# Depthwise convolution of a transformer block: from seven tiles on TensorE and one on VectorE to eight on TensorE, with shifted copies made by DMA

## The chip, the cores and the metric

The kernel runs on one core of one Trainium2 chip. The metric is the device time of the execution in microseconds (us). Every run of the kernel before is given below; the profile is of one more execution.

## The reference

Two transformer blocks are computed on 256 positions of 1024 channels, batch 1, in float32. The change lies in the first block, in a conformer convolution module, between its first pointwise product and its second:

```python
def causal_dwconv(x, w):
    k, ch = w.shape
    return lax.conv_general_dilated(
        x, w[:, None, :].astype(x.dtype), window_strides=(1,), padding=[(k - 1, 0)],
        dimension_numbers=("NWC", "WIO", "NWC"), feature_group_count=ch)

def conformer_conv_module(h, w1, b1, dw_w, dw_b, ln_g, ln_b, w2, b2):
    u = h @ w1 + b1
    a, gt = jnp.split(u, 2, axis=-1)
    u = a * jax.nn.sigmoid(gt)
    u = causal_dwconv(u, dw_w) + dw_b
    u = jax.nn.silu(layernorm(u, ln_g, ln_b))
    return u @ w2 + b2

...
    c_act = jax.nn.silu(c)
    mod = c_act @ mod_w[i] + mod_b[i]
    h = rmsnorm(x, norm_pre_mix[i]) * (1.0 + sc_m) + sh_m
```

The convolution has 31 taps per channel. The vector `mod` holds 6 x 1024 scales and shifts; the first two sixths are needed for `h`, the third after the module, the others later. The rest (a feed-forward part with a 3-tap convolution, and a second block with an RWKV mixer, a stick-breaking attention and four more feed-forward parts) is not touched.

## The kernel before

Activations lie with channels on the partitions: a tile is 128 channels x 256 positions, and there are eight (`KD`). Weights stream from HBM in chunks of 1 MB. Since TensorE multiplies in a reduced float32 format here, each half chunk ("unit", 128 x 1024) is split in two: `split_hi` is a cast on ScalarE (L226) and `split_lo` the remainder, a subtraction on VectorE (L235); after every second `split_lo` the next chunk is loaded by SyncE (L204). A product is three matmuls (high x high, high x low, low x high).

The order of the work is the order in which the Python program emits it; every engine runs its own instructions strictly in that order, and so does SyncE with the loads. There is no scheduler.

The matrix behind `mod` is read in 48 tiles `mraw` of 512 KB through five buffers. For each tile VectorE multiplies it with silu(c) (`mod_mult`, L720), ScalarE sums it (`mod_sum`, L724), and then the buffer is loaded again (`mod_load`, L733). One such sum and the next multiply together form a "half" in `mod_later`; halves are put on a list `bg`, and `pump` takes them from it at given places.

The module in the order of its stages:

- First pointwise product, `pw1(k)` for k = 0 to 7 (L1009): 48 matmuls per step into eight PSUM banks. In each step VectorE and ScalarE also make the step's operand (L986, L1031, L1033, L1034, L1045), split two units and do two tiles of `mod`. After step 1 SyncE loads `taps` (L1051); after step 2 GpSimd builds five of the tap matrices `stack` (`conv_stack`, L906, 128 x 1024 each); after step 5 the vectors `vecs` (L663) and the constants are loaded.
- Gate: per tile a sigmoid on ScalarE (L1099) and a multiply on VectorE (L1101) that writes `up`.
- Convolution: tile 0 runs on VectorE in one scaling (L1084) and 30 tap steps (L1088). Tiles 1 to 7 run on TensorE: `shifts` (L1072) multiplies with slices of the identity to bring `up` in four shifts onto the four groups of 32 partitions, ScalarE copies that out of PSUM into `sh` (L1076), and 32 matmuls (L1128) with the tap matrix sum up the taps. ScalarE writes the result with its bias (L1139) and its square (L1331). Two more tap matrices are built when a buffer is free. Between the matmuls `pump` issues 22 halves of `mod` and the tap steps in turn. Five `split_hi` are placed in the last tiles, four `split_lo` after the stage.
- Norm: sums over channels by TensorE (L1383), VectorE and ScalarE make mean and deviation (L1394 to L1405), TensorE broadcasts them (L1408); `keep_warm` issues six filler matmuls before and six after that (L360).
- Second pointwise product: five groups of tiles are normed (L1161), passed through silu (L1167) and split into the operand `xx` (L625, L626). `gemm_square` takes the first four tiles one by one and the last four in `gemm_tail`; the results are read from PSUM on VectorE (L1179), and squared. After the fourth tile `pump` issues the last three halves and the next splits of the memory input `mx`.

Of the kernel before, what the change touches and what calls it, by code (L numbers as in the profile page):

```python
# [23 lines left out]
N_PE_CONV = 7  # L24
N_STACK = 5
MOD_LATE = 3
PUMPS = {3: 3}
CV = (5, 4)
# [3 lines left out]
CONV_ORDER = [4, 5, 0, 1, 2, 3, 6, 7]  # L32
# [218 lines left out]
class Builder:  # L251
# [6 lines left out]
    def __init__(self, ctx, tc, dr, out, parts):  # L258
        self.tc, self.nc, self.dr, self.out = tc, tc.nc, dr, out
        self.parts = parts  # L260
        self.npool = 0
        e = ctx.enter_context
        self.const = e(tc.tile_pool(name="const", bufs=1))
        self.wraw = e(tc.tile_pool(name="wraw", bufs=self.RAW))
        self.whi = e(tc.tile_pool(name="whi", bufs=self.LEAD + 3))
        self.wlo = e(tc.tile_pool(name="wlo", bufs=self.LEAD + 2))
        self.act = e(tc.tile_pool(name="act", bufs=1))
        self.ps_gu = e(tc.tile_pool(name="ps_gu", bufs=2, space=PSUM))
        self.xr = self.act.tile([P, KD, T], F32, name="xr")
# [3 lines left out]
        self.bg = []  # L273
        self.pre = None
# [41 lines left out]
    def enter_dense(self, tmp=True):  # L316

        self.dense = ExitStack()
        self.ps_st = self.dense.enter_context(self.pool("ps_st", PSUM))
        self.ps_acc = self.dense.enter_context(self.pool("ps_acc", PSUM))  # L320
        if tmp:
            self.open_tmp()

# [3 lines left out]
    def leave_dense(self):  # L327
        self.dense.close()
# [408 lines left out]
    def mod_later(self, first, last):  # L737

        def half(n):
            if n > 2 * first:  # L740
                self.mod_sum(self.mod_raw.pop(0), n - 1)
                self.mod_load(1)
            if n < 2 * last:
                self.mod_mult(self.mod_raw[0])

        for n in range(2 * first, 2 * last + 1):
            self.bg.append((1.1, lambda n=n: half(n)))
# [162 lines left out]
    def conformer(self):  # L910
        with self.pool("conf") as cp:
            st, later = self.pointwise_conv(cp)
        self.pointwise_out(st, later)

    def pointwise_conv(self, cp):
# [5 lines left out]
        junk = self.acc_tile(0)[:, 0, :]  # L921
# [76 lines left out]
        npe, ndv = N_PE_CONV, KD - N_PE_CONV  # L998
        first = [j for j in order if j >= ndv]

        banks = [self.acc_tile(i) for i in range(4)] + [self.gu_tile(), self.gu_tile()] + [
# [18 lines left out]
        for k in range(KD):  # L1020
# [39 lines left out]
        ups = [cp.tile([P, (3 if j >= ndv else CW - 1) + T], F32, name=f"up{j}") for j in range(KD)]  # L1060
        for t in ups:
            nc.vector.memset(t[:, :-T], 0.0)

        def shifts(j):

            out = []
            for h in range(2):
                ps = self.gu_tile()
                for s in range(4):
                    for q in range(2):  # L1070
                        c = 64 * h + 32 * q
                        nc.tensor.matmul(ps[32 * s:32 * s + 32, q, :], lhsT=self.k("ident")[:, c:c + 32],  # L1072
                                         rhs=ups[j][:, 3 - s:3 - s + T], start=True, stop=True,
                                         skip_group_check=True)
                sh = cp.tile([P, 2, T], F32, name="sh", bufs=4)
                nc.scalar.copy(out=sh, in_=ps)  # L1076
                out.append(sh)
            return out

        def conv_dve(j):  # L1080
            y = self.ys[:, j, 0, :]

            def first():
                nc.vector.tensor_scalar(out=y, in0=ups[j][:, 0:T], scalar1=self.vec("a_dw_w", j),  # L1084
                                        scalar2=self.vec("a_dw_b", j), op0=ALU.mult, op1=ALU.add)

            def tap(t):
                nc.vector.scalar_tensor_tensor(out=y, in0=ups[j][:, t:t + T],  # L1088
                                               scalar=self.vec("a_dw_w", t * 8 + j), in1=y,
                                               op0=ALU.mult, op1=ALU.add)  # L1090
            return [first] + [lambda t=t: tap(t) for t in range(1, CW)] + [
                lambda: st.square(j, j + 1)]

        taps = []
        sh = {}
        for j in order:
# [4 lines left out]
            nc.vector.scalar_tensor_tensor(out=ups[j][:, -T:], in0=gu[:, 0, :], scalar=self.vec("a_pw1_b", j),  # L1101
                                           in1=sg, op0=ALU.add, op1=ALU.mult)
            if j < ndv:
                taps.append(conv_dve(j))

        self.mod_later(8, 20)
        n = len(self.bg) - MOD_LATE
        mods, later, steps = self.bg[:n], self.bg[n:], list(zip(*taps))
        self.bg = []
        for i, step in enumerate(steps):  # L1110
            for f in step:
                self.bg.append((0.4, f))
            if mods:
                self.bg.append(mods.pop(0))
        for j in range(ndv):
            self.bg.append((0.65, lambda j=j: st.sum(j, j + 1, "dve")))
        self.bg += mods
        self.mark("conv")
        slot = sum(c for c, _ in self.bg) / (4 * npe)
        sh[first[0]] = shifts(first[0])  # L1120
        done = []
        for n, j in enumerate(first):
            if n + 1 < npe:
                sh[first[n + 1]] = shifts(first[n + 1])
            cv = self.acc_tile(n % 4)[:, 0, :]
            for a in range(8):
                for g in range(4):
                    nc.tensor.matmul(cv[32 * g:32 * g + 32, 4 * a:], lhsT=stacks[n][:, 8 * g + a, :],  # L1128
                                     rhs=sh[j][g // 2][:, g % 2, :T - 4 * a], start=a == 0,
                                     stop=a == 7, skip_group_check=True)  # L1130
# [4 lines left out]
            if n + N_STACK < npe:  # L1135
                stacks.append(self.conv_stack(cp, first[n + N_STACK]))
            if done and n < npe - 1:
                st.sum(done[-1], done[-1] + 1, "dve")
# [3 lines left out]
            done.append(j)  # L1142
        self.pump(1000)
        for j in done[-2:]:
            st.sum(j, j + 1, None)
        return st, later

    def pointwise_out(self, st, later):
# [15 lines left out]
        for i, (k0, k1) in enumerate(groups):  # L1164
# [6 lines left out]
            if i in LOS:  # L1171
                self.stream.split_hi()
                self.stream.split_lo()
# [145 lines left out]
class Norm:  # L1319
# [40 lines left out]
    def finish(self, eps, func, ahead=True, fill=(0, 0)):  # L1360
# [6 lines left out]
        b.fill(fill[0], b.WARM0)  # L1367
        bc = next(parts)
        b.fill(fill[1], b.WARM)
# [924 lines left out]
```

## Time and profile before

| | us |
|---|---|
| three runs | 1485.37, 1481.81, 1486.15 |
| median | 1485.37 |
| the profiled execution | 1481.87 |
| span of the profiled execution, first to last instruction | 1480.1 |
| first conv instruction on TensorE | 72.97 |
| broadcast of the norm's values | 125.66 |
| last operand of the second product | 143.11 |
| first read of its result | 148.26 |

The profile lists engines as PE (TensorE), PEld (its weight loads), DVE (VectorE), ACT (ScalarE), POOL (GpSimd) and SP (SyncE, the loads). A timeline row gives the start, the duration, the engine, the line, the operation and the tiles written and read; "x5" means that many instructions in one row, and what stands in square brackets is the idle time before it and what ended it. On VectorE and ScalarE the tail of one instruction overlaps the start of the next by about 0.1 us. PEclk is the granted TensorE clock, 1.00 for 2.4 GHz and 0.50 for 1.2 GHz.

### The profile page before, as it was taken

The page shows a single profiled execution, that of the slowest core. Times are in us where ns is not written, and L with a number is a line of the kernel's source. Part 1 is how long each engine was busy: PE and PEld are TensorE (multiplying, and loading weights), DVE is VectorE, ACT ScalarE, POOL GpSimd, SP SyncE. Part 2 cuts the span into 40 slices and gives each one's busy share as a digit, 9 for nine tenths or more (in the row PEclk, how much of TensorE's full clock was granted, in tenths as well). Part 3 has the DMA queues.
Part 4 walks back from the last instruction along what each step waited for, and adds up shares of the span by engine and source line. Part 5 has one row for each costly group of instructions (what it writes and reads, how often), then busy time and mean ns, then how long its engine had stood idle before and what let it go on. Part 6 is the DMA issues. An engine that isn't in the chain of part 4 may idle for free. (4 is left out here: it accounts for less than half of the span.)

```text
span 1480.1 us, 26075 instructions
## 1 busy us (share of the span) xinstructions
PE 1419.9 (96%) x10664; PEld 1273.4 (86%) x10664; DVE 1076.0 (73%) x1705; ACT 853.8 (58%) x1505; POOL 119.6 (8%) x113
## 2 busy tenths in 40 slices
PE   8888899999999999999999999999999999999997
PEld 7867799998888888898788888888888888888886
DVE  7897788885777656788568776678766765787754
ACT  6787566684655535751346555466554676565542
POOL 1210100001000010031010000110001111100011
PEclk9998899999999999999999999999999999999998
DMA  9774445565355553240024555536554342265540
GB/s 379 292 243 186 170 155 189 198 234 207 136 202 179 196 199 136 86 143 4 2 109 167 184 196 181 189 143 221 182 195 187 136 143 86 91 226 196 196 174 29
DMA packets 39145, 250.38 MB, mean 169 GB/s; under 512 B 4337, under 2 KB 4849, under 8 KB 12274
## 3 DMA queue, kind: packets, MB, share of 16 engines
q1 hardware_dynamic: 38594, 247.60, 45.9%
q8 instruction: 84, 1.38, 0.4%
q10 hardware_dynamic: 432, 1.11, 0.2%
q14 instruction: 35, 0.29, 0.1%
HBM read 247.65 MB, written 1.05 MB: 168 GB/s over the span
## 5 line engine op out<-in xcount | busy, mean ns | idle before, releaser
L235 DVE TENSOR_TENSOR wlo<-wraw,whi 128x1024 fp32r<-128x1024 f32 x416 | 514.3, 1250 | 34.1 <-ACT whi L226 33.4
L226 ACT CAST whi<-wraw 128x1024 fp32r<-128x1024 f32 x416 | 426.3, 1045 | 22.0 <-PE acc L378 5.6
L384 PE MATMUL acc<-hx,whi 128*128 128x512 f32 x880 | 310.7, 398 | 0.0
L384 PE MATMUL acc<-xx,whi 128*128 128x512 f32 x816 | 284.1, 390 | 0.0
L372 PE MATMUL acc<-xx,wlo 128*128 128x256 f32 x1008 | 280.7, 284 | 0.0
L372 PE MATMUL gu<-xx,wlo 128*128 128x256 f32 x1008 | 279.0, 282 | 1.6 <-ACT xx L625 1.0
L372 PE MATMUL acc<-hx,wlo 128*128 128x256 f32 x880 | 247.5, 281 | 0.0
L384 PEld LDWEIGHTS acc<-hx,whi 128*128 128x128 f32 x880 | 165.3, 188 | 40.5
L372 PEld LDWEIGHTS gu<-xx,wlo 128*128 128x128 f32 x1008 | 189.9, 189 | 4.9 <-ACT xx L625 1.7
L372 PEld LDWEIGHTS acc<-xx,wlo 128*128 128x128 f32 x1008 | 190.9, 191 | 0.8
L384 PEld LDWEIGHTS acc<-xx,whi 128*128 128x128 f32 x816 | 153.2, 188 | 32.1
L372 PEld LDWEIGHTS acc<-hx,wlo 128*128 128x128 f32 x880 | 166.1, 189 | 0.0
L384 PE MATMUL gu<-xx,whi 128*128 128x512 f32 x432 | 150.9, 390 | 0.0
L377 PE MATMUL gu<-xx,whi 128*128 128x256 f32 x512 | 148.4, 290 | 2.4 <-ACT u L894 2.4
L378 PE MATMUL gu<-xx,whi 128*128 128x256 f32 x512 | 142.9, 279 | 0.0
L1331 ACT ACTIVATE ys<-ys 128x256 f32<-128x256 f32 (+1 forms) x66 | 28.6, 437 | 151.7 <-DVE ys L1249 134.9
L377 PEld LDWEIGHTS gu<-xx,whi 128*128 128x128 f32 x512 | 96.2, 188 | 10.8 <-issue 7.9
L378 PEld LDWEIGHTS gu<-xx,whi 128*128 128x128 f32 x512 | 96.3, 188 | 0.7 <-issue 0.7
L384 PEld LDWEIGHTS gu<-xx,whi 128*128 128x128 f32 x432 | 81.1, 188 | 17.0
L1348 POOL TENSOR_TENSOR nsum<-ys 128x512 f32<-128x512 f32 (+1 forms) x9 | 12.4, 1380 | 871.1 <-PE acc L384 452.3
L858 ACT COPY lows<-acc 128x256 f32<-128x256 f32 x55 | 20.6, 374 | 97.8 <-PE acc L384 97.6
L1247 DVE SCALAR_TENSOR_TENSOR ys<-xr,acc 128x256 f32<-128x256 f32 x32 | 13.5, 422 | 75.0 <-PE acc L384 75.0
(397 smaller groups left out, 2351.5 us busy)
## 6 DMA issues: line engine op xcount, KB each, us to landing
wraw<-in_w SPq DMA_DIRECT2D x208, 1024.0 KB, 4.8
mraw<-in_mod SPq DMA_DIRECT2D x48, 512.0 KB, 5.5
xr<-in_x SPq DMA_DIRECT2D x2, 512.0 KB, 4.2
m<-in_mem SPq DMA_DIRECT2D x1, 1024.0 KB, 8.2
out<-xr SPq DMA_DIRECT2D x3, 256.0 KB, 2.2
cst<-in_consts SPq DMA_DIRECT2D x1, 546.0 KB
lora<-in_lora ACTq DMA_DIRECT2D x1, 384.0 KB, 3.4
lora_g<-in_lora ACTq DMA_DIRECT2D x1, 384.0 KB, 3.9
```

The lines of the kernel that those rows point to most:

```text
L226: b.nc.scalar.copy(out=hi, in_=raw)
L235: b.nc.vector.tensor_tensor(out=lo, in0=raw, in1=hi.bitcast(F32), op=ALU.subtract)
L372: self.nc.tensor.matmul(out, lhsT=wl, rhs=x[:, 0, :], start=start, stop=False, skip_group_check=True)
L377: mm(out, lhsT=wh, rhs=x[:, 0, :], start=start, stop=False, skip_group_check=True)
L378: mm(out, lhsT=wh, rhs=x[:, 1, :], start=False, stop=False, skip_group_check=True)
L384: self.nc.tensor.matmul(bank, lhsT=wh, rhs=x, start=False, stop=stop, skip_group_check=True)
L858: nc.scalar.copy(out=lows[:, 1, :], in_=banks[1][:, 1, :])
L1247: self.nc.vector.scalar_tensor_tensor(out=y, in0=self.xr[:, k, :], scalar=2 * ALPHA, in1=ps[:, 1, :], op0=ALU.mult, op1=ALU.add)
L1331: b.nc.scalar.activation(out=b.ys[:, k0:k1, 1, :], in_=y, func=AF.Square)
L1348: e.tensor_tensor(out=out[:, q:2, :], in0=prev[:, q:2, :], in1=t[:, q:2, :], op=ALU.add)
```

## The change

All eight tiles are convolved on TensorE, in the order 4, 5, 0, 2, 1, 3, 6, 7. The first three get their shifts from TensorE as before. The other five lie in one tile `upd`, and 16 DMAs of 160 KB (`shifts_dma`, four for each shift) copy it within SBUF into `shd`. Four tap matrices are kept instead of five, and the first four are built after step 6 of the first product; the taps are loaded after step 5, vecs and consts after step 6. silu(c) is copied into two PSUM banks (`pair`) for the multiplies of the convolution stage (`mod_mult_psum`). 18 halves of `mod` are issued there and seven in the second product, two after each of its first four tiles. Three `split_lo` stand between the last conv tiles instead of four after them. The norm's filler matmuls become 18 and 22. The accumulator banks are reopened after the stage.

```diff
-N_PE_CONV = 7
-N_STACK = 5
-MOD_LATE = 3
-PUMPS = {3: 3}
-CV = (5, 4)
+N_STACK = 4
+CONV_ORDER = [4, 5, 0, 2, 1, 3, 6, 7]
+N_DMA = 5
+MOD_LATE = 7
+PUMPS = {0: 2.2, 1: 2.2, 2: 2.2, 3: 2.2}
...
+    def mod_mult_psum(self, raw):
+
+        self.nc.vector.tensor_tensor(out=raw, in0=raw, in1=self.cps, op=ALU.mult)
+
...
+        upd = cp.tile([P, N_DMA, 3 + T], F32, name="upd")
+        ups = [cp.tile([P, 3 + T], F32, name=f"up{n}") for n in range(KD - N_DMA)]
+        for t in ups:
+            nc.gpsimd.memset(t[:, :3], 0.0)
+        nc.gpsimd.memset(upd[:, :, :3], 0.0)
+        ups += [upd[:, n, :] for n in range(N_DMA)]
...
-            if k == 1:
+            if k == 5:
                 nc.sync.dma_start(out=self.taps, in_=self.dr["taps"])
-            elif k == 2:
-                stacks = [self.conv_stack(cp, j) for j in first[:N_STACK]]
-            elif k == 5:
+            elif k == 6:
                 self.load_consts()
+                stacks = [self.conv_stack(cp, j) for j in order[:N_STACK]]
...
+        shd = cp.tile([P, N_DMA, 4, T], F32, name="shd")
+
+        def shifts_dma(s):
+
+            for g in range(4):
+                nc.sync.dma_start(out=shd[32 * s:32 * s + 32, :, g, :],
+                                  in_=upd[32 * g:32 * g + 32, :, 3 - s:3 - s + T])
...
+        self.cps = pair.rearrange("p a t -> p (a t)")
+        for h in range(2):
+            c = slice(512 * h, 512 * h + 512)
+            nc.scalar.copy(out=self.cps[:, c], in_=self.cact[:, c])
...
                 if a % 2:
                     self.pump(slot)
-            if n >= npe - CV[0]:
+                    if n < 1:
+                        shifts_dma(a // 2)
+            if 3 <= n:
                 self.stream.split_hi()
...
+            if 4 <= n < KD - 1:
+                self.stream.split_lo()
...
-        for _ in range(CV[1]):
-            self.stream.split_lo()
-        bc = st.finish(LN_EPS, AF.Silu, False)
+        bc = st.finish(LN_EPS, AF.Silu, False, warm=(18, 22))
...
             if i in LOS:
+                self.stream.split_lo()
                 self.stream.split_hi()
-                self.stream.split_lo()
```

SyncE at the end of the first product and in the convolution, before (`mraw` are the tiles of `mod`, `wraw` the weight chunks):

```order
L204 DMA wraw<-in_w 128x2048
L663 DMA vecs<-in_vecs 128x710
L664 DMA cst<-in_consts 128x1092
L733 DMA mraw<-in_mod 128x1024
L204 DMA wraw<-in_w 128x2048
L733 DMA mraw<-in_mod 128x1024 x2
L204 DMA wraw<-in_w 128x2048
L733 DMA mraw<-in_mod 128x1024 x22
L204 DMA wraw<-in_w 128x2048 x3
```

and of the change:

```order
L203 DMA wraw<-in_w 128x2048
L1069 DMA taps<-in_taps 128x288
L742 DMA mraw<-in_mod 128x1024
L203 DMA wraw<-in_w 128x2048
L668 DMA vecs<-in_vecs 128x710
L669 DMA cst<-in_consts 128x1092
L742 DMA mraw<-in_mod 128x1024 x2
L203 DMA wraw<-in_w 128x2048
L742 DMA mraw<-in_mod 128x1024
L1097 DMA shd<-upd 32x5x256 x4
L742 DMA mraw<-in_mod 128x1024
L1097 DMA shd<-upd 32x5x256 x4
```

The taps load stands where the vecs load stood, and four copies stand before each of the next loads of `mod` (two more such pairs follow, then 14 loads in a row).

VectorE in the second product, from the last operand `xx` to the first reads of the result `ys`, before:

```order
L626 TENSOR_TENSOR xx<-ys,xx 128x2x256
L235 TENSOR_TENSOR wlo<-wraw,whi 128x1024
L720 TENSOR_TENSOR mraw<-mraw,cact 128x1024 x2
L235 TENSOR_TENSOR wlo<-wraw,whi 128x1024
L1179 TENSOR_SCALAR ys<-acc_1481,vecs 128x256 x2
```

and of the change:

```order
L631 TENSOR_TENSOR xx<-ys,xx 128x2x256
L725 TENSOR_TENSOR mraw<-mraw,cact 128x1024 x4
L234 TENSOR_TENSOR wlo<-wraw,whi 128x1024
L725 TENSOR_TENSOR mraw<-mraw,cact 128x1024 x2
L234 TENSOR_TENSOR wlo<-wraw,whi 128x1024
L631 TENSOR_TENSOR mx<-m,mx 128x2x256 x2
L234 TENSOR_TENSOR wlo<-wraw,whi 128x1024
L1179 TENSOR_SCALAR ys<-acc_1418,vecs 128x256 x2
```

Four multiplies, one weight split and two splits of the memory input more stand ahead of the first read.

## Rows read from the trace of the kernel before

**Rows 1.** The page, first part: busy time, share of the span, instructions.

```profile
PE 1419.9 (96%) x10664; PEld 1273.4 (86%) x10664; DVE 1076.0 (73%) x1705; ACT 853.8 (58%) x1505; POOL 119.6 (8%) x113
```

**Rows 2.** Timeline of TensorE: start, us, engine, line, operation, tiles, count [idle before].

```profile
72.41 0.28 PE L1009 MATMUL bc<-xx,wlo 128*128 128x256 f32 x1
...
72.76 0.28 PE L1009 MATMUL bc<-xx,wlo 128*128 128x256 f32 x1
72.97 3.80 PE L1072 MATMUL gu<-up,head 128*32 128x256 f32 x64
...
79.81 1.98 PE L1072 MATMUL gu<-up,head 128*32 128x256 f32 x32
81.55 3.52 PE L1128 MATMUL acc<-sh,stack 128*32 128x256 f32 x64
...
125.66 1.12 PE L1408 MATMUL bc<-head,rn 128*128 128x128 f32 x4 [2.16 <-DVE rn L1401]
...
152.10 0.38 PE L377 MATMUL acc<-xx,whi 128*128 128x256 f32 x1 [1.02 <-DVE ys L1179]
```

**Rows 3.** Timeline of GpSimd in the first product.

```profile
32.41 12.15 POOL L906 TENSOR_TENSOR stack<-taps 128x1024 f32<-128x1024 f32 x5 [31.96 <-DMA taps<-in_taps]
```

**Rows 4.** Timeline of VectorE in the first product.

```profile
34.87 2.93 DVE L235 TENSOR_TENSOR wlo<-wraw,whi 128x1024 fp32r<-128x1024 f32 x1
...
63.31 1.22 DVE L235 TENSOR_TENSOR wlo<-wraw,whi 128x1024 fp32r<-128x1024 f32 x1
...
65.71 0.42 DVE L1045 TENSOR_TENSOR xx<-ys,xx 128x256 fp32r<-128x256 f32 x1 [1.11 <-ACT xx L1034]
```

**Rows 5.** Windows of 2.5 us: busy time of each engine, PEclk, DMA share, GB/s.

```profile
42.50:45.00 2.50, 2.17 (x10) 2.17 (x11) 2.50 (x2) 1.11 (x3) 2.05 (x1) 0.50 0.16 25
...
47.50:50.00 2.50, 2.50 (x23) 2.50 (x23) 2.50 (x5) 1.56 (x3) 0.00 (x0) 1.00 0.83 243
```

**Rows 6.** Timeline of ScalarE in the convolution.

```profile
78.38 1.05 ACT L724 ACTIVATE mraw<-mraw 128x1024 f32<-128x1024 f32 x1
...
81.28 1.15 ACT L1076 COPY sh<-gu 128x512 f32<-128x512 f32 x2
...
114.75 1.04 ACT L226 CAST whi<-wraw 128x1024 fp32r<-128x1024 f32 x1
...
120.40 0.47 ACT L1139 ACTIVATE ys<-acc,vecs 128x256 f32<-128x256 f32 x1
120.89 0.42 ACT L1331 ACTIVATE ys<-ys 128x256 f32<-128x256 f32 x1
```

**Rows 7.** Timeline of VectorE in the convolution and the norm.

```profile
74.30 1.22 DVE L720 TENSOR_TENSOR mraw<-mraw,cact 128x1024 f32<-128x1024 f32 x1
...
113.99 4.12 DVE L1088 SCALAR_TENSOR_TENSOR ys<-up,vecs,ys 128x256 f32<-128x256 f32 x8
...
120.20 4.63 DVE L235 TENSOR_TENSOR wlo<-wraw,whi 128x1024 fp32r<-128x1024 f32 x4
124.74 0.34 DVE L1394 SCALAR_TENSOR_TENSOR sd<-st,msq 128x1 f32<-128x1 f32 x2
```

**Rows 8.** Timeline of VectorE in the second product.

```profile
143.11 0.69 DVE L626 TENSOR_TENSOR xx<-ys,xx 128x512 fp32r<-128x512 f32 x1 [1.81 <-ACT xx L625]
...
144.85 2.35 DVE L720 TENSOR_TENSOR mraw<-mraw,cact 128x1024 f32<-128x1024 f32 x2
...
148.26 0.87 DVE L1179 TENSOR_SCALAR ys<-acc,vecs 128x256 f32<-128x256 f32 x2
```

**Rows 9.** Timeline of SyncE in the first product.

```profile
54.32 0.42 SPq L663 DMA_DIRECT2D vecs<-in_vecs  x1
```

**Rows 10.** DMA issues: tiles, count, KB each, median us from issue to landing.

```profile
mraw<-in_mod SPq DMA_DIRECT2D x48, 512.0 KB, 5.5
...
vecs<-in_vecs SPq DMA_DIRECT2D x1, 355.0 KB, 8.2
...
out<-xr SPq DMA_DIRECT2D x2, 128.0 KB, 2.0
```

More of the change, by code (lines that the diff above doesn't have):

```diff
@@ L912, in conformer @@
             st, later = self.pointwise_conv(cp)
+        self.accs.close()
+        self.open_acc()
         self.pointwise_out(st, later)
@@ L920, in pointwise_conv @@
         nc.vector.memset(warm.bitcast(F32), 0.0)
-        junk = self.acc_tile(0)[:, 0, :]
+        pair = self.ps_acc.tile([P, 4, T], F32, name="pair")
+        junk = pair[:, 0, :]
         def keep_warm(n):
@@ L997, in pointwise_conv @@
         order = CONV_ORDER
-        npe, ndv = N_PE_CONV, KD - N_PE_CONV
-        first = [j for j in order if j >= ndv]
-        banks = [self.acc_tile(i) for i in range(4)] + [self.gu_tile(), self.gu_tile()] + [
+        upd = cp.tile([P, N_DMA, 3 + T], F32, name="upd")
[4 more added lines that the diff above has]
+        ups += [upd[:, n, :] for n in range(N_DMA)]
+        banks = [pair[:, 0:2, :], pair[:, 2:4, :]] + [self.acc_tile(i) for i in range(2)] + [
+            self.gu_tile(), self.gu_tile()] + [
             self.ps_st.tile([P, 2, T], F32, name=nm, tag=nm) for nm in ("st", "bc")]
@@ L1059, in pointwise_conv, with shifts @@
         st = Norm(self, True)
[L1060 to L1066, printed above, removed]
+        def shifts(n):
+            sh = cp.tile([P, 4, T], F32, name="sh", bufs=2)
             for h in range(2):
@@ L1072, in shifts @@
                         nc.tensor.matmul(ps[32 * s:32 * s + 32, q, :], lhsT=self.k("ident")[:, c:c + 32],
-                                         rhs=ups[j][:, 3 - s:3 - s + T], start=True, stop=True,
+                                         rhs=ups[n][:, 3 - s:3 - s + T], start=True, stop=True,
                                          skip_group_check=True)
[L1075 to L1096, printed above, removed]
+                nc.scalar.copy(out=sh[:, 2 * h:2 * h + 2, :], in_=ps)
+            return sh
+        shd = cp.tile([P, N_DMA, 4, T], F32, name="shd")
[3 more added lines that the diff above has]
+                                  in_=upd[32 * g:32 * g + 32, :, 3 - s:3 - s + T])
+        for n, j in enumerate(order):
             gu = banks[j]
@@ L1100, in pointwise_conv @@
                                  bias=self.vec("a_pw1_b", 8 + j))
-            nc.vector.scalar_tensor_tensor(out=ups[j][:, -T:], in0=gu[:, 0, :], scalar=self.vec("a_pw1_b", j),
+            nc.vector.scalar_tensor_tensor(out=ups[n][:, -T:], in0=gu[:, 0, :], scalar=self.vec("a_pw1_b", j),
                                            in1=sg, op0=ALU.add, op1=ALU.mult)
-            if j < ndv:
-                taps.append(conv_dve(j))
+        self.cps = pair.rearrange("p a t -> p (a t)")
+        for h in range(2):
+            c = slice(512 * h, 512 * h + 512)
+            nc.scalar.copy(out=self.cps[:, c], in_=self.cact[:, c])
         self.mod_later(8, 20)
[L1107 to L1117, printed above, removed]
-        self.mark("conv")
[L1119 to L1125, printed above, removed]
+        n = len(self.bg) - 2 * (MOD_LATE // 2) - 1
+        later, self.bg = self.bg[n:], self.bg[:n]
+        self.mark("conv")
+        slot = sum(c for c, _ in self.bg) / (4 * KD - 4)
+        sh = [shifts(0)]
+        for n, j in enumerate(order):
+            if n + 1 < KD - N_DMA:
+                sh.append(shifts(n + 1))
+            cv = self.acc_tile(n % 2)[:, 0, :]
+            x = sh[n] if n < KD - N_DMA else shd[:, n - KD + N_DMA]
             for a in range(8):
@@ L1141, in pointwise_conv @@
             st.square(j, j + 1)
-            done.append(j)
+            if n and n < KD - 1:
+                i = order[n - 1]
+                st.sum(i, i + 1, "dve")
         self.pump(1000)
-        for j in done[-2:]:
+        for j in order[-2:]:
             st.sum(j, j + 1, None)
+        self.cps = None
         return st, later
```

29 lines of the change are left out of this document (16 added, 13 removed).

## The prediction

> **What bounds the kernel now.** I read the page first: TensorE is busy for 96% of the span [rows 1], so time can be won only where it waits or runs at its lower clock, and outside the first 165 us the change edits nothing. There I read three stages, engine by engine, in the timelines. All clock times below are us from the span's start in the trace of the kernel before.
>
> In the first pointwise product (to 72.97, the first conv instruction [rows 2]) VectorE is stopped by GpSimd. GpSimd builds five tap matrices in one block of 12.15 us from 32.41 [rows 3]; a weight split that takes 1.22 us later on takes 2.93 inside that block [rows 4]. Five such stops of 1.71 us make 8.5 us. TensorE starves behind them: at 42.5 to 45 its clock is 0.50 (1.2 GHz) with 10 instructions in 2.5 us, at 47.5 to 50 it is 1.00 with 23 [rows 5].
>
> In the convolution (72.97 to the last square's end, 120.89 + 0.42 = 121.31 [rows 6], so 48.34 us) VectorE is the late engine: 22 multiplies of 1.22 and 31 tap steps of 4.12 / 8 = 0.52 [rows 7] are 43 us, with four weight splits behind them, and TensorE's 7 tiles of 3.52 and 7 shifts of 1.98 [rows 2] are 39.
>
> In the second pointwise product the operands end at 143.11 + 0.69 = 143.80; VectorE then works without a gap (one split, two multiplies, one split) until it takes the first result at 148.26 [rows 8], and TensorE waits 1.02 us for such a read at 152.10 [rows 2]. VectorE is again the late one.
>
> **Part A, tap matrices built at the end of the first product.** The taps load moves from the second step to the sixth, and GpSimd builds four matrices once it lands. What this removes is the 8.5 us of stops. TensorE needs 16 groups of three matmuls, 0.35 us apart (72.41 to 72.76 [rows 2]), 5.6 us, per step, so it began its last step at about 67.4; its operand was ready at 65.71 + 0.42 = 66.13 [rows 4]. The slack is 1.2 us.
>
> What it adds: the taps are now issued where the vecs load stood, at 54.32 [rows 9], and vecs took 8.2 us to land [rows 10]. So the matrices begin at about 62.5 on the old clock, just when VectorE does the last step: split, scaling, split (63.31), bias, operand (65.71). All of these are instructions of the kinds that were stopped. Four stops of 1.71 are 6.8 us; 1.1 of it falls into VectorE's own wait before 65.71 [rows 4] and 1.2 into the slack, so 4.5 us reach TensorE. An idle gap of that length was followed by clock 0.50 [rows 5]; that costs between 0 and 2.7 us (the 13 instructions missing from a 2.5 us slice, at 0.12 each, for up to two slices, less what was idle), and I take 1.4. A = 8.5 - 4.5 - 1.4 = **+2.6 us** gained. The ends are -1.0 (8.5 - 6.8 - 2.7) and +8.5 (the matrices miss VectorE).
>
> **Part B, the convolution.** Gone from VectorE are the 31 tap steps and 4 of 22 multiplies; 18 multiplies, five sums and three splits leave about 28 us, so VectorE no longer sets the pace. TensorE gets one tile more and four shifts fewer: 8 x 3.52 + 3 x 1.98 = 34 us. The new bound is ScalarE, whose queue holds 17 sums of 1.05, eight copies of 1.15 / 2 (six of shifts, and the two that put silu(c) into PSUM, priced the same as the nearest row), eight tile results of 0.47 and squares of 0.42, five splits of 1.04 [rows 6]: 17.9 + 4.6 + 7.1 + 5.2 = 34.8 us. With 0.6 us of the last sigmoid before it and about 1 us behind the first shifts the floor is 36.5 us.
>
> Above the floor lie waits for loads. A sum frees its buffer, the load takes 5.5 us [rows 10], the multiply 1.22, and only then can the sum five places later run. Into the same SyncE queue the change puts 16 copies, four after each of the first four loads. At about 0.4 us per issue and 0.55 us of transfer each (160 KB; the upper price is 1.0, from 2.0 us for a 128 KB output [rows 10] of which I count half as latency) the loads for halves 21 to 24 land 9, 12.5, 16 and 19.5 us after the start instead of one after each sum. Carried through ScalarE's queue this adds 6 us: the last square ends 42.4 us after the start, against 48.34: +5.9. Ends: 37.5 (loads keep up) and 46 (copies take 0.8 each). A multiply with one operand in PSUM has no row; VectorE has over 10 us to spare, so up to 0.5 us more for each of 18 would stay hidden behind ScalarE, and a saving would bring nothing.
>
> The four splits that held VectorE from 120.20 until the norm's first step at 124.74 [rows 7] are taken out of the way, so the norm's broadcast, at 125.66 [rows 2], 4.35 us after the last square, comes 3.1 us after it (about 1.0 for the sums, then 18 filler matmuls of 0.117): +1.25. The fillers cost nothing while the clock is 1.00, 1.7 us if it is 0.50. B = **+7.2 us** (3.6 to 12.1).
>
> The Trainium skill has a rule against this part: SBUF — State Buffer, section "SBUF: two separate sides", under "Door 1", says a transfer that touches 32 partitions reaches only eight of the sixteen DMA ports. Every one of the 16 copies writes 32 partitions; no row shows such a transfer. By an estimate from that rule the copies run at half rate, the last square comes at about 45.7 and the result is 1482.8 instead of 1479.5, which is still the forecast's case.
>
> **Part C, the second product.** Four halves more of the modulation move here. Between the last operand and the first result read VectorE now has six multiplies instead of two, three splits instead of two, and two splits of the memory input that used to come after all results: 4 x 1.18 (2.35 / 2) + 1.22 + 2 x 0.69 = 7.3 us more [rows 8]. Nothing covers it, since VectorE was already the late engine there; TensorE waits first for the split weights and then for the reads that free its banks. The two memory splits are missing later: -1.4. The last two multiplies need loads that start only when ScalarE has done the first sum of this stage, and the memory splits wait for ScalarE behind seven sums: 0 to 2.5, I take 1.5. A gap of over 4 us on TensorE may lower its clock again: 0 to 2.3, I take 0, as its last tiles wait for VectorE anyway. C = **-7.4 us** (-5.9 to -10.7).
>
> Bank names, the order of tiles 1 and 2, the memsets moved to GpSimd and the later vecs and consts cost nothing: TensorE's last step and the idle GpSimd cover them; vecs, landing about 3 us before the first sigmoid, would cost what it is late.
>
> **Sum.** 2.6 + 7.2 - 7.4 = 2.4 us. Against the profiled execution's own 1481.87 us that is 1479.5. That execution stands 3.5 us below the median of the three runs (1485.37) and beside the fastest (1481.81), so I name **1480**. A measurement of this kernel can tell about 0.3% (4.4 us) from no change, and 2.4 is inside it.
>
> **The rivals.** *The matrices miss VectorE*: the taps land after 65 on the old clock, or GpSimd loses the turns. For it: loads were dense there and landings vary; against: the vecs row. Then A is 8.5 and the time 1473.6. *The loads keep up*: the copies slip between loads; ScalarE runs at its floor, B is 12.1, the time 1474.6. For it: the page's slowest loads are not typical; against: SyncE issues in order and four copies stand ahead of each early load. *The copies are served one by one* (slower): each takes the 2.0 us that the 128 KB output shows [rows 10], the sixteenth lands 33 us after the start, and five tiles of 3.3 us still follow: the last square at 51. B is -1.4, the sum -6.2, the time 1488.1. It decides from about 1.9 us per copy on. *PSUM does not part VectorE from GpSimd* (the change does not do what it says): the four later matrices stop four multiplies by 1.71 each, of which about half reaches ScalarE: 1483. The same page and section of the Trainium skill says the lock concerns VectorE instructions with two inputs in SBUF; the stops in [rows 4] are of that kind, and no row shows one with a PSUM input beside GpSimd.
>
> **Chances.** Forecast 0.44, matrices miss 0.20, loads keep up 0.18, copies one by one 0.12, PSUM does not part them 0.06. So faster by over 0.3%: 0.38; within: 0.50; slower: 0.12. The range reaches from below both faster cases to the slow one: 1471 to 1488.
>
> **What would show it.** Right for A: GpSimd's first matrix in the last or next-to-last step, instructions of about 2.9 us on VectorE there, conv starting at about 70.4. Right for B: ScalarE without long gaps except for multiplies of halves 21 to 26, and the first tile from copies waiting for a DMA or not at all; the broadcast about 45.5 us after the conv's start. Right for C: the first result read 29 to 32 us after the broadcast instead of 22.6, with TensorE idle before it. The forecast is wrong if conv starts near 64.5, if the copies land after 25 us, or if the reads in C come no later than before.

## The result and the profile after

The change makes the kernel slower: 1495.38 us median (1494.06 to 1496.40, four runs) against 1483.83 us (1481.81 to 1486.15) of the kernel before, a ratio of 1.0079 with a 95% interval of 1.0061 to 1.0097. The forecast was 1480 with a range of 1471 to 1488, so the time lies outside it; slower had been given 0.12. The profiled execution took 1496.4 us with a span of 1494.4, 14.3 more than before.

Four marks, read from the timelines, place those 14.3 us:

| | before | after | forecast | after minus before |
|---|---|---|---|---|
| A: first conv instruction | 72.97 | 70.50 | 70.4 | -2.5 |
| last square, us after that | 48.34 | 54.25 | 42.4 | +5.9 |
| broadcast, us after that | 4.35 | 3.87 | 3.1 | -0.5 |
| C: first result read, us after that | 22.60 | 31.86 | 29 to 32 | +9.3 |

These add up to 12.2 us. Part A came as worked out and part C inside its range. Part B, the convolution with its norm, lost 5.4 us where 7.2 were to be won. The forecast had a gain of 2.4; of the 14.6 us between that and the marks, B makes 12.6, C 1.9 and A 0.1.

The page's first part, busy time by engine, answers [rows 1]:

```profile
PE 1422.4 (95%) x10628; PEld 1272.6 (85%) x10628; DVE 1058.3 (71%) x1666; ACT 854.0 (57%) x1500; POOL 119.4 (8%) x118
```

VectorE has 17.7 us less work than before and the kernel is longer: less work on it does not by itself shorten the path.

TensorE's timeline after, as [rows 2], from the last step of the first product to the broadcast:

```profile
62.21 0.38 PE L1027 MATMUL gu<-xx,whi 128*128 128x256 f32 x1 [1.81 <-ACT xx L1052]
63.27 0.39 PE L1027 MATMUL gu<-xx,whi 128*128 128x256 f32 x1 [0.67 <-DVE xx L1063]
...
70.50 1.97 PE L1086 MATMUL gu<-up,head 128*32 128x256 f32 x32
...
96.75 7.00 PE L1125 MATMUL acc<-shd,stack 128*32 128x256 f32 x64 [9.98 <-DMA shd<-upd]
105.65 3.47 PE L1125 MATMUL acc<-shd,stack 128*32 128x256 f32 x64 [1.89 <-ACT ys L1138]
...
128.62 0.60 PE L1409 MATMUL bc<-head,rn 128*128 128x128 f32 x4
```

The first tile that comes from a DMA copy is waited for 9.98 us, until 26.2 us after the conv's start, later than the 25 us that the prediction named as a sign of being wrong. The tile itself then takes 7.00 us instead of 3.47: its first matmuls still wait for copies, the last of which lands at 99.08, 28.6 us after the start, and the granted clock is 0.50 from 92 to 101.

ScalarE's last square, which ends the stage:

```profile
124.33 0.42 ACT L1331 ACTIVATE ys<-ys 128x256 f32<-128x256 f32 x1
```

GpSimd and VectorE at the end of the first product, as [rows 3] and [rows 4]; first GpSimd, whose bracket says that it had been idle for 52.52 us until the taps landed, 7.7 us after their issue at 45.69:

```profile
53.46 9.46 POOL L915 TENSOR_TENSOR stack<-taps 128x1024 f32<-128x1024 f32 x4 [52.52 <-DMA taps<-in_taps]
```

and VectorE beside it, later in the convolution (four multiplies with their load waits), and in the second product:

```profile
54.29 2.14 DVE L999 SCALAR_TENSOR_TENSOR ys<-xr,head,rms 128x256 f32<-128x256 f32 x1
56.35 2.93 DVE L234 TENSOR_TENSOR wlo<-wraw,whi 128x1024 fp32r<-128x1024 f32 x1
59.21 1.87 DVE L1049 TENSOR_TENSOR mod<-mod,sbias 128x2 f32<-128x2 f32 x1
62.19 1.02 DVE L1063 TENSOR_TENSOR xx<-ys,xx 128x256 fp32r<-128x256 f32 x1 [1.11 <-ACT xx L1052]
...
81.13 1.22 DVE L729 TENSOR_TENSOR mraw<-mraw,pair 128x1024 f32<-128x1024 f32 x1 [2.68 <-DMA mraw<-in_mod]
89.12 1.22 DVE L729 TENSOR_TENSOR mraw<-mraw,pair 128x1024 f32<-128x1024 f32 x1 [6.77 <-DMA mraw<-in_mod]
96.04 1.22 DVE L729 TENSOR_TENSOR mraw<-mraw,pair 128x1024 f32<-128x1024 f32 x1 [5.70 <-DMA mraw<-in_mod]
100.21 5.00 DVE L729 TENSOR_TENSOR mraw<-mraw,pair 128x1024 f32<-128x1024 f32 x4 [2.95 <-DMA mraw<-in_mod]
105.13 1.23 DVE L1348 TENSOR_TENSOR nsum<-ys 128x512 f32<-128x512 f32 x1
...
145.58 0.69 DVE L631 TENSOR_TENSOR xx<-ys,xx 128x512 fp32r<-128x512 f32 x1 [1.82 <-ACT xx L630]
146.18 4.63 DVE L725 TENSOR_TENSOR mraw<-mraw,cact 128x1024 f32<-128x1024 f32 x4
150.73 1.22 DVE L234 TENSOR_TENSOR wlo<-wraw,whi 128x1024 fp32r<-128x1024 f32 x1
153.19 2.50 DVE L725 TENSOR_TENSOR mraw<-mraw,cact 128x1024 f32<-128x1024 f32 x2 [1.25 <-DMA mraw<-in_mod]
155.60 1.22 DVE L234 TENSOR_TENSOR wlo<-wraw,whi 128x1024 fp32r<-128x1024 f32 x1
158.14 1.29 DVE L631 TENSOR_TENSOR mx<-m,mx 128x512 fp32r<-128x512 f32 x2 [1.31 <-ACT mx L630]
159.35 1.22 DVE L234 TENSOR_TENSOR wlo<-wraw,whi 128x1024 fp32r<-128x1024 f32 x1
160.48 0.87 DVE L1179 TENSOR_SCALAR ys<-acc,vecs 128x256 f32<-128x256 f32 x2
```

In the last step a split of 1.22 us takes 2.93 again, and two others grow by 1.66 and 1.71: the matrices do collide with VectorE. In the convolution VectorE waits for loads of `mod`. In the second product six groups of work stand between the last operand and the first read, where the kernel before has three.

The DMA issues on the page after (count, KB each, median us to landing) and the windows that hold the copies, with one of the first product for comparison (last two columns: share of the 16 transfer engines, GB/s):

```profile
shd<-upd SPq DMA_DIRECT2D x16, 160.0 KB, 7.2
```

```profile
40.00:60.00 20.00, 20.00 (x174) 20.00 (x173) 20.00 (x21) 14.80 (x24) 6.54 (x3) 1.00 1.00 392
...
84.00:90.00 6.00, 2.77 (x56) 2.18 (x48) 0.88 (x1) 0.00 (x1) 3.47 (x2) 1.00 1.08 236
90.00:96.00 6.00, 0.00 (x0) 0.00 (x0) 0.34 (x1) 1.93 (x4) 0.00 (x0) 0.61 1.12 192
```

Loads alone fill the engines at 392 GB/s; with the copies among them they are as full and move 192 to 236.

The remaining 2.1 us of the span lie behind the changed stages. Both kernels wait 2.4 us for the same operand in the next stage. Before, the clock stayed at 1.00 there (first row, of before); after, it was granted 0.83 in the window at the same distance (second row):

```profile
205.00:215.00 10.00, 9.19 (x79) 9.22 (x80) 8.25 (x15) 6.42 (x12) 0.00 (x0) 1.00 0.59 217
```

```profile
217.20:227.20 10.00, 9.14 (x66) 9.17 (x67) 8.25 (x15) 6.38 (x12) 0.00 (x0) 0.83 0.62 215
```

Thirteen matmuls of 0.12 us fewer in it are 1.6 us. This is one execution; the medians differ by 11.6 us, close to the 12.2 of the marks.

### The profile page after: what moved, and what is told of

The parts are those of the page before. It is cut to its first block, busy times and chain, and to the rows that moved or that the text cites. A ratio compares the mean times of both kernels' runs of the same rounds, so it can differ in the third digit from the quotient of the medians.

```text
span 1494.4 us, 25995 instructions
## 1 busy us (share of the span) xinstructions
PE 1422.4 (95%) x10628; PEld 1272.6 (85%) x10628; DVE 1058.3 (71%) x1666; ACT 854.0 (57%) x1500; POOL 119.4 (8%) x118
```

## The experiments

Each kernel is the changed kernel with the edit shown, unless it says otherwise. "Last square" is counted from the conv's start, "first read" from the broadcast. A kernel that ran once has no interval.

**What in the convolution is late?** First (e1) the copies were left out (`x = sh[min(n, KD - N_DMA - 1)]`, no `shifts_dma`).

> The changed kernel without its 16 copies; the five tiles that used them are convolved with the shifts of the third tile, so the result is not the reference's and the amount of work on TensorE stays. Changed kernel's marks: conv starts at 70.5, last square ends 54.25 us later, broadcast 58.1 us after the start. Theory (the copies take the transfer time that the loads of mod need, and hold their own tiles): last square 38 to 41 us after the start, time about 1480. Rival (ScalarE's queue, the multiplies with a PSUM operand or the clock set the stage, the copies only come beside it): last square 48 us or more after the start, time above 1489.

Last square 42.89, time 1486.62 beside 1483.17 of before. Neither number was met: it lies between the two theories, the last square 11.4 us below the changed kernel's and 2 to 5 above the theory's, the time of this one run 8.8 below. The waits of ScalarE in the stage, after and then in this kernel (total us, times, longest):

```profile
ACT mraw L733 <- DVE mraw L729: 14.9, 4, 6.4
```

```profile
ACT ys L1130 <- PE acc L1119: 3.7, 3, 1.4
ACT mraw L733 <- DVE mraw L729: 2.7, 5, 0.7
```

So the copies cost the stage 11.4 us, as late loads for ScalarE's sums (14.9 us of waits against 2.7). Without any copy the stage is still 6.4 us above the 36.5 us floor, which is what the prediction allowed for loads and copies together; of this 2.7 are waits for multiplies, and 3.7 are waits for TensorE's tiles, for which the prediction had no term.

Then (e2) all tiles were shifted by TensorE, without the copies:

```diff
-            if n + 1 < KD - N_DMA:
+            if n + 1 < KD:
                 sh.append(shifts(n + 1))
...
-            x = sh[n] if n < KD - N_DMA else shd[:, n - KD + N_DMA]
+            x = sh[n]
```

> The changed kernel with all eight tiles shifted by TensorE and copied by ScalarE, no copies by DMA. Theory (copies are the loss): ten more ScalarE copies of 0.58 us and five more shifts of 1.98 on TensorE, so the last square comes 44 to 47 us after the conv's start instead of 54, time about 1485 to 1487. Rival (the loss lies elsewhere in the stage): 54 us plus some of the added work, 56 to 60, time 1497 or more.

Last square 46.16, time 1487.18 (1.0019, 1.0001 to 1.0037). As the theory said, the time just above its range: the ten ScalarE copies and five shifts that the DMA copies save cost 3.3 us, the DMA copies 11.4.

**Why are the copies so dear?** One row per partition instead of five (e3):

```diff
-                nc.sync.dma_start(out=shd[32 * s:32 * s + 32, :, g, :],
-                                  in_=upd[32 * g:32 * g + 32, :, 3 - s:3 - s + T])
+                nc.sync.dma_start(out=shd[32 * s:32 * s + 32, g, :row],
+                                  in_=flat[32 * g:32 * g + 32, 3 - s:3 - s + row])
...
```

> The changed kernel with the same 16 copies between the same groups of 32 partitions, but each partition's part as one row of 5.2 KB (the five tiles and the gaps between them in one piece) instead of five rows of 1 KB. Theory of rows (a row costs a fixed time: 1 KB rows took 84 to 108 ns each where a 4 KB row of a load took 159): the copies are done about 12 to 15 us after the conv's start instead of 26, last square 40 to 44 us after it, time about 1483. Theory of partitions (writing 32 partitions halves the rate, whatever the rows): copies done after 24 us or later, last square 52 us or more after the start, time 1493 or more.

Landing and last square hardly changed (7.8 and 53.44), 1498.16 us (1.0098, 1.0073 to 1.0123). The theory of rows fell.

```profile
shd<-upd SPq DMA_DIRECT2D x16, 161.5 KB, 7.8
```

All 128 partitions on both sides (`out=shd[:, g, s, :], in_=upd[:, g, 3 - s:3 - s + T]`, with a fifth such copy for each `s`, 20 in all, e4):

> The changed kernel with 20 copies of 128 KB, each from all 128 partitions to all 128 partitions, in rows of 1 KB as before: the same bytes and rows, but the wrong partitions, so the result is not the reference's. Theory of rows: no change, copies done about 26 us after the conv's start, last square 52 to 56 us after it, time 1493 to 1497. Theory of partitions: copies done after 12 to 16 us, last square 41 to 46, time 1482 to 1486.

```profile
shd<-upd SPq DMA_DIRECT2D x20, 128.0 KB, 3.9
```

Landing 3.9, last square 48.08, time 1488.75: the direction of the theory of partitions, short of its 41 to 46 and 1482 to 1486. That kernel had another number and size of copies, so two more kept both and moved only the partitions (`shd[s::4]` from `upd[g::4]`, then `shd[s::4]` from the 32 neighbours of the change; e13, e14).

> The changed kernel with the same 16 copies of 32 partitions to 32 partitions, 160 KB in rows of 1 KB, but every fourth partition of 128 instead of 32 neighbours, on both sides; the result is not the reference's, since the channels go to the wrong places. Theory (32 neighbouring partitions lie on half of the ports, so spreading them gives the rate back): copies land in 3.5 to 5 us (changed kernel 7.2, with all partitions in each copy 3.9), last square 46 to 50 us after the conv's start, time 1484 to 1490. Rival (the number of partitions or of copies counts, not where they lie; all 128 in one copy was faster for that): landing 6.5 us or more, last square 52 to 56, time 1492 to 1498.

> The same with only the written partitions spread over all 128 and the read ones 32 neighbours, as in the changed kernel; the result is not the reference's. If the written side sets the rate: landing 3.5 to 5 us, last square 46 to 50 us after the conv's start, time 1484 to 1490. If the read side sets it: landing 6.5 us or more, last square 52 to 56, time 1492 to 1498. If both sides count: between.

Both sides spread, then the written side alone:

```profile
shd<-upd SPq DMA_DIRECT2D x16, 160.0 KB, 4.0
```

```profile
shd<-upd SPq DMA_DIRECT2D x16, 160.0 KB, 4.1
```

Last square 46.99 and 48.68, times 1484.19 and 1490.80 (before 1483.87; the first also began its convolution 3.6 us earlier than the second, at 66.42, in part A, and the second's time is just above its range). Same bytes, rows and count, and the copies land in 4.0 us instead of 7.2: where the written partitions lie sets how fast they land. This is the rule that the prediction weighed, the Trainium skill, SBUF — State Buffer, "SBUF: two separate sides", "Door 1": the number of ports that the partitions reach decides, and 32 neighbours reach half. The landings agree with it (7.2 against 4.0, a factor of 1.8). So does the time of a single row of 1 KB in the traces from 72 to 99 us, 89 ns in the mean in the changed kernel and 48 in e13.

Of the 11.4 us that the copies cost the stage, spreading gives back 7.3 (e13) and 5.6 (e14). The rest stays: ScalarE still waits longer for multiplies than the 2.7 us without copies, here in e13:

```profile
ACT mraw L733 <- DVE mraw L729: 8.4, 5, 3.4
```

Even spread, then, the copies cost 4.1 to 5.8 us, no less than TensorE's shifts with 3.3.

Last (e11), the copies in ScalarE's queue (`nc.scalar.dma_start`), so that no load stands behind one in SyncE's:

> The changed kernel with its 16 copies issued by ScalarE instead of SyncE, so that no load of mod is queued behind a copy. Theory (the copies hold the loads in the transfer itself): loads of mod still take 8 to 11 us to land while the copies run, TensorE still waits over 6 us for its first copied tile, last square 50 to 56 us after the conv's start, time 1490 to 1497. Rival (the order in SyncE's queue is the loss): loads land in 5 to 6 us, ScalarE loses the 16 issues instead, last square 44 to 48 us after the start, time 1484 to 1488.

```profile
83.24 4.10 ACTq L1097 DMA_DIRECT2D shd<-upd x3
87.39 1.06 ACT L733 ACTIVATE mraw<-mraw 128x1024 f32<-128x1024 f32 x1 [4.78 <-DMA mraw<-in_mod]
...
93.67 0.47 ACT L1138 ACTIVATE ys<-acc,vecs 128x256 f32<-128x256 f32 x1 [5.13 <-issue]
```

Last square 54.71, time 1496.1, as the theory said. The three loads that were issued while copies were under way, at 79.9, 82.6 and 88.6, took 6.8, 9.5 and 10.4 us to land, and the four issued from 96.6 to 99.7, after the last copy's issue, 5.2 to 5.9. So loads are late beside the copies with no copy in their own queue, and the order in SyncE's queue is not needed for it. But ScalarE was held by its own issues as well, and TensorE waited 11.09 us for ScalarE's copy of the third tile's shifts where the theory had a wait for a copied tile. How much the queue's order adds in the changed kernel stays open; moving the copies does not help.

**Is VectorE the wait in the second product?** The four halves put back (`MOD_LATE = 3`, `PUMPS = {3: 3}`; e5):

> The changed kernel with the four halves of mod put back into the convolution stage (three left for the second product, after its fourth tile, as before). In the changed kernel the first result read comes 31.9 us after the broadcast, before 22.6. Theory (VectorE's added work ahead of the first read is that loss): the read comes 23 to 25 us after the broadcast; the conv stage gets four more sums of 1.05 and loads behind the copies, its last square at 55 to 59 us instead of 54.3; time about 1488 to 1492. Rival (TensorE waits there for weights or a tile that is late anyway): the read stays at 29 us or more after the broadcast, time 1495 or more.

```profile
147.24 0.69 DVE L631 TENSOR_TENSOR xx<-ys,xx 128x512 fp32r<-128x512 f32 x1 [1.81 <-ACT xx L630]
...
150.12 2.36 DVE L725 TENSOR_TENSOR mraw<-mraw,cact 128x1024 f32<-128x1024 f32 x2
152.39 1.22 DVE L234 TENSOR_TENSOR wlo<-wraw,whi 128x1024 fp32r<-128x1024 f32 x1
153.52 0.87 DVE L1179 TENSOR_SCALAR ys<-acc,vecs 128x256 f32<-128x256 f32 x2
```

First read 23.22 us after the broadcast, last square 54.27, time 1491.65 (1.0052, 1.0033 to 1.0071). Part C is shown: 8.6 of its 9.3 us come back. The convolution, which waits for its copies, ends its last square no later with the four halves, but the broadcast comes 5.41 us behind it instead of 3.87, as the 18 fillers took 3.69 us instead of 2.40. The time falls by less than the mark, 3.7 us in the medians (7.4 between the two profiled executions).

The other way, one half left (`MOD_LATE = 1`, `PUMPS = {3: 3}`, on the kernel of e8 below; e12):

> The kernel with TensorE's shifts, the late matrices and three late halves (1476.8 us), with only one half of mod left for the second product and two more in the convolution. Theory (each multiply ahead of the first read costs its 1.18 us there and a sum of 1.05 in the convolution): first read 20.5 to 22 us after the broadcast instead of 23.7, last square 48 to 49 us after the start instead of 46.4, time 1475.5 to 1478. Rival (the convolution has room for them): last square at 46 to 47, time 1473.5 to 1475.5.

```profile
143.15 2.50 DVE L631 TENSOR_TENSOR mx<-m,mx 128x512 fp32r<-128x512 f32 x4 [3.19 <-ACT mx L630]
```

First read 26.64, last square 49.53, time 1479.49 (0.9975, 0.9960 to 0.9990): slower than with three halves, which no theory said. The pump fills its place with what stands next in the list, and that is the splits of the memory input, whose load had not landed: VectorE waits 3.19 us ahead of the first read for ScalarE's cast of it, which itself waits 2.02 us for the load. The list decides what comes there, not only how much.

**Do the tap matrices hold VectorE?** The taps' load behind vecs and consts (e6):

```diff
-            if k == 5:
-                nc.sync.dma_start(out=self.taps, in_=self.dr["taps"])
-            elif k == 6:
+            if k == 6:
                 self.load_consts()
+                nc.sync.dma_start(out=self.taps, in_=self.dr["taps"])
                 stacks = [self.conv_stack(cp, j) for j in order[:N_STACK]]
```

> The changed kernel with the load of the taps issued behind vecs and consts, at about 52 us instead of 45.7, so that GpSimd builds its four matrices from about 60 on, behind VectorE's last step of the first product. Theory (the builds stop VectorE there and TensorE starves): no VectorE instruction of 2.9 us in the last step, TensorE keeps its clock of 1.00 from 60 to 68, the conv starts at 66 to 67 instead of 70.5; time about 1490 to 1492, if the first tile need not wait for its matrix. Rival (the last step waits for something else): conv starts at 69.5 or later, time 1494 or more.

GpSimd's builds and one window of the last step (after: clock 0.52 at 65 to 67.5):

```profile
61.89 7.54 POOL L915 TENSOR_TENSOR stack<-taps 128x1024 f32<-128x1024 f32 x4 [60.95 <-DMA taps<-in_taps]
```

```profile
62.50:65.00 2.50, 2.50 (x24) 2.50 (x23) 0.88 (x3) 0.95 (x3) 2.50 (x2) 1.00 0.80 329
```

Conv start 65.85 without a stop, time 1489.30 (1.0042, 1.0030 to 1.0054), both just below the theory's. The collision cost 4.65 us.

**Does PSUM part VectorE from GpSimd?** The copies of silu(c) into `pair` left out, so that the multiplies read SBUF (e7):

> The changed kernel without the two copies of silu(c) to PSUM: the multiplies of the convolution read it from SBUF as before. Theory (a PSUM operand parts VectorE from GpSimd, but VectorE has slack): multiplies beside the four later matrix builds take about 2.9 us instead of 1.22, and the time stays within 4 us of 1495. Rival (PSUM makes no difference to the stops): no multiply differs from the changed kernel's 1.22 us, time 1493 to 1496.

GpSimd, after and then in this kernel, and VectorE in this kernel:

```profile
103.90 1.91 POOL L915 TENSOR_TENSOR stack<-taps 128x1024 f32<-128x1024 f32 x1 [15.08 <-PE acc L1125]
```

```profile
104.02 1.91 POOL L915 TENSOR_TENSOR stack<-taps 128x1024 f32<-128x1024 f32 x1 [15.42 <-PE acc L1121]
```

```profile
104.61 3.53 DVE L725 TENSOR_TENSOR mraw<-mraw,cact 128x1024 f32<-128x1024 f32 x2 [1.38 <-DMA mraw<-in_mod]
```

Of the two multiplies the first starts beside a build that lasts until 105.93 and takes 2.40 us, the second, behind the build, 1.21. In the changed kernel the last of the four from 100.21 on lies beside the build at 103.90 (103.99 to 105.21) and takes 1.22, while the sum behind it, with both operands in SBUF, takes 1.23 instead of 0.68. PSUM does part them. Only this one of the four later builds met a multiply over most of its length, and the stop is 1.2 us where the theory had 1.7. The time of this one run, 1498.80, is inside the theory's 4 us.

**Do the three repairs add up?** TensorE's shifts (e2), three late halves (e5) and late matrices (e6) together, as e8:

> The changed kernel with TensorE's shifts for all tiles (no copies), the four halves of mod back in the convolution stage and the taps' load behind vecs and consts. Theory (these three are the losses, and they add up): conv starts at 66 to 67, last square 47 to 51 us later, broadcast 5 us after that, first read 23 to 25 us after the broadcast: 143 to 147 against 148.3 before; time 1477 to 1481, against 1483.2 before. Rival (they share a bound, so that what one gives another takes): time within 3 us of the run with TensorE's shifts alone, 1484 to 1490.

Conv start 65.82, last square 46.42, broadcast 4.81 later, first read 23.68 after it, at 140.73. Time 1476.79 (0.9948, 0.9927 to 0.9968), below the kernel before, and like the last square and the first read a little below the theory's range. They add up: singly the three take 8.2, 3.7 and 6.1 us off the changed kernel's median, together 18.6. No kernel varies the option `dynamic_dma_scratch_size=1024`, which the change also sets.

The kernel before with late matrices alone (e9):

> The kernel before with one edit: vecs, consts and the taps are loaded after step 6 of the first product, in this order, and GpSimd builds its five matrices from about 61 us on. The convolution stays as it was, with tile 0 on VectorE and silu(c) in SBUF. Theory (the stops are moved, not removed: VectorE's multiplies and tap steps read two operands from SBUF, and the builds last until about 73): conv starts at 66, but two or three multiplies beside the builds take about 2.9 us, and since VectorE is late in that stage the last square comes 50 to 53 us after the start instead of 48.3; time 1478 to 1481 against 1483.0. Rival (the stage absorbs them, the gain of 7 us is whole): last square 48 to 49 us after the start, time 1475 to 1477.

```profile
66.71 2.93 DVE L720 TENSOR_TENSOR mraw<-mraw,cact 128x1024 f32<-128x1024 f32 x1
...
72.63 2.13 DVE L1086 SCALAR_TENSOR_TENSOR ys<-up,vecs,ys 128x256 f32<-128x256 f32 x1
```

Conv start 64.89, last square 50.38, time 1477.47 (0.9963, 0.9949 to 0.9977). The stops move into the convolution, as the theory said (a multiply at 2.93, two tap steps at 2.13), and the time is a little below its range. This one move gives 5 us, most of the 6.2 that e8 has.

Last, e8 with the norm's fillers of before (`warm=(6, 6)`; e10):

> The kernel with TensorE's shifts, the late matrices and three late halves (1476.8 us, run before this one) with 6 filler matmuls ahead of the norm's broadcast and 6 behind it, as the kernel before has, instead of 18 and 22. There the 18 took 3.36 us, the broadcast came 4.81 us after the last square and the second product began at clock 1.00. Theory (fillers on the path): broadcast about 3 to 3.4 us after the last square, the second product starts 1.5 to 3 us earlier, time 1474 to 1476. Rival (without them the clock is low at the start of the second product, as in the kernel before from 128.8 to 132.6): first read no earlier, time 1476 to 1479.

TensorE, with 18 and with 6 fillers:

```profile
113.90 3.36 PE L365 MATMUL gu<-whi 128*128 128x256 f32 x18
117.05 1.06 PE L1400 MATMUL bc<-head,rn 128*128 128x128 f32 x4
```

```profile
116.07 0.95 PE L365 MATMUL gu<-whi 128*128 128x256 f32 x6
117.38 0.65 PE L1400 MATMUL bc<-head,rn 128*128 128x128 f32 x4 [0.35 <-DVE rn L1393]
...
120.06 0.58 PE L382 MATMUL acc<-xx,whi 128*128 128x256 f32 x1 [0.90 <-ACT xx L630]
```

1472.75 us (0.9927, 0.9910 to 0.9945), the fastest kernel here and below both theories. The broadcast comes 2.96 us after the last square instead of 4.81. But the second product starts at a granted clock of 0.50 (120 to 124), and the first read is at 140.64, no earlier than 140.73, since this execution's convolution was 2.3 us longer. The runs of the two kernels do not overlap (1471.53 to 1474.81, 1475.07 to 1479.14), but in the two profiled executions the difference arises far behind the edit: between two norms' broadcasts, from 555 us on, e8's takes 215.4 us and e10's 210.2. That the fillers are its cause stays open.

## Why the prediction was wrong

**Part A: right in the mechanism, and in the number by luck, as two errors cancel.** The conv's start was put at 70.4 and came at 70.50; the taps landed beside the last step as reckoned. But what the removal gives is 7.1 us (72.97 to e6's 65.85), not 8.5, and the collision takes 4.65 back, not 5.9. The stops were 1.66, 1.71, 1.71 and 0.60, TensorE waited 2.5 us for them, and the clock fell. In the nine other kernels with this placement the start was at 69.5 to 71.3 eight times and once at 66.4 (e13), where the builds caught one instruction fewer; that they miss VectorE altogether, which had 0.20, never came.

**Part B: wrong, in the term of the copies.** ScalarE's work was sized well: 54.25 less its 18.6 us of waits for multiplies (14.9), tiles (2.7) and shifts (1.0) is 35.7, against 34.8 for its queue and 36.5 for the floor. The step that failed is the wait above the floor, put at 6 us for loads and copies together; the stage ended 17.75 us above it. Without any copy it is 6.4 (e1: 2.7 for multiplies, 3.7 for TensorE's tiles), so "loads keep up" at 37.5, which had 0.18, was not reached even then, and the copies add 11.4. I priced one at 0.55 us, for which I gave no row, with an upper end of 1.0 taken from an output to HBM. The first four loads behind the copies let their multiplies begin 10.6, 18.6, 25.5 and 29.7 us after the start where the loads were to land at 9, 12.5, 16 and 19.5: 8.0, 6.9 and 4.2 us apart instead of 3.5. In the trace the copies of a group land about 1.0 us apart (89.46, 90.40, 91.59, 92.50), and the load behind them 3.4 us later; spread over the partitions, in e13, they land 0.46 apart (82.04, 82.50, 82.96, 83.41). So the price of 0.55 was too low for copies into 32 neighbouring partitions. An issue also took 0.67 us instead of 0.4; what that adds was not separated.

The rule of the Trainium skill that I weighed and set beside the sum was right, and its effect larger than my estimate of 45.7: spreading gives back 5.6 to 7.3 us, where I had added 3.3. The slow rival had the direction, with 51 and a chance of 0.12, but not the price: it needed about 1.9 us for each copy and the last to land 33 us after the start, and it was 1.0 and 28.6. What it left out is that the loads among the copies slow down too, and ScalarE's sums with them.

**The norm: nearly nothing.** The broadcast came 3.87 us after the last square, 0.5 us sooner instead of 1.25. The 18 fillers of 0.12 us stand there; where the clock is low they cost more (3.36 us in e8, at a granted 0.50). In e1, e2, e5, e6 and e8 the broadcast came 4.79 to 5.41 us after the last square, later than the 4.35 before.

**Part C: right, and it was the largest loss.** VectorE needs 14.2 us from the end of the last operand to the first read instead of 4.5: 4.8 more of multiplies, 1.2 of splits, 1.3 for the memory splits and 2.6 of waits for a load and a cast. The operand came 0.5 earlier; 9.3 remain, against 7.4 with a range to 10.7. The 1.4 us that I credited for memory splits missing later did not come: from the first read to the next norm's first step both kernels take 29.8 us.

**The sum.** That PSUM would not part VectorE from GpSimd is refuted (e7). With the forecast's own A and C and nothing for B the sum would have been 2.6 - 7.4 = -4.8, and the prediction 1486.7 and slower: the gain rested on B.

## What to carry to other kernels

Work that is moved out of a late engine is worth only what the engine that takes it can spare: DMA copies inside SBUF are not free when the same transfer engines feed the stage, and copies that write 32 neighbouring partitions took nearly twice as long to land as the same bytes spread out (7.2 against 4.0 us). Even spread they were no cheaper here than the shifts on TensorE that they replace. Move work only to a place where its engine isn't the one waited for; the four halves cost 2 us each ahead of the first read, and left the last square where it was in a stage that waits anyway. When a change bundles several moves, price the one that helps by itself: here a later load of the taps alone takes 5 us off the kernel before, and the rest of the change loses more than that.

## What the runs showed of the hardware that was not expected

- Five times longer rows (5.2 KB instead of 1 KB) did not speed up a copy within SBUF at all: 7.8 against 7.2 us to landing. The written partitions did: 4.0 to 4.1 when every fourth one is written, 3.9 with all 128. With the read ones left as neighbours it stayed at 4.1, so the written side decides here; the read side spread alone was not run.
- Beside the copies into neighbouring partitions the transfer engines show full (share 1.08 to 1.12) at 192 to 236 GB/s, where loads alone reach 392 at a share of 1.00.
- A multiply with one operand in PSUM takes 1.22 us, like one with both in SBUF, and still 1.22 beside a GpSimd build; with both in SBUF one took 2.40 there.
